# A mixer-and-MLP trunk in fp32 products of three matmuls: projections four k tiles ahead of the attention, the second half of q and k split earlier, and smaller edits to the first stage

## The chip, the cores and the metric

The kernel runs on one core of a Trainium2 chip. The metric is the device time of one execution in microseconds (us), lower is better, as the median of several runs. A profile of one execution, taken by the hardware profiler, goes with it. Differences of under 0.2% of the time, some 5 us, are not told apart here.

## What is computed

Two layers over a sequence of 1024 positions of width 1024, batch 1, all in float32. Layer 0 mixes tokens by forgetting attention (16 heads of 64), layer 1 by a chunked spatial gate; each is followed by a convolutional gated MLP of width 2816. The change lies in layer 0's first half:

```python
mod = silu(c) @ ada_w[0] + ada_b[0]            # shift, scale, gate, twice
h = rmsnorm(x, norm1_g[0]) * (1 + sc1) + sh1
q, k, v, o, fl = split(h @ w_in)               # q, k, v, o of width 1024, fl of 16
q, k = rmsnorm per head of 64, with gains
F = cumsum(log_sigmoid(fl + b_f))              # over positions
logits = q k^T / 8 + F[t] - F[s], causal
att = softmax(logits) @ v
x = x + gate * ((att * sigmoid(o)) @ w_out)
```

## The kernel before

TensorE multiplies float32 numbers that are split in two: `hi` is the number rounded to the format fp32r that TensorE reads, `lo` is the rest. `mm3` (L108) makes a product of three matmuls, hi by hi, hi by lo and lo by hi. `pair` and `split_lo` (L119 to L136) make the two parts: a copy on ACT, a subtraction on DVE. The cost of a split therefore falls on ACT and DVE, and TensorE waits for it where no other work lies ready.

**First stage.** `xn` holds the 8 row tiles of x. Each is squared on ACT with a sum (L319), groups of tiles then get their reciprocal root on DVE (`rstd`, `rsqrt`, L321 and L138, three Newton steps of small instructions), are scaled (L467) and transposed by TensorE (L469). `ada_first(q)` (L415), four times, multiplies a quarter of the first modulation matrix by `silu(c)` on DVE: eight row blocks of 512 columns, which arrive in two pieces of 1 MB or, for the tag `pt`, two halves of a piece. `raw_pieces` (L403) names the buffer for each of the 8 pieces. The buffers are those that the attention uses later (`qq`, `kh`, `kl`, `pt`) and the two of `w`; a piece that takes a buffer again has to wait until DVE has read the piece before. Then h is scaled, shifted and split (L494 to L496), and the o projections of three column blocks start (`acc`, L498).

**Attention.** Heads go in pairs, p = 0 to 7, two heads of 64 on the 128 partitions. For each pair `proj` (L566) makes q, k and v by 8 tiles of 128 positions in two halves, each tile a sum of 8 k tiles (three matmuls each, `pj`). After the fourth tile of a half, q and k are normalised: a square on ACT (L592), a sum on DVE (L594), the small Newton instructions, and a product on DVE (L600). `heads_qk(rw, half)` (L690) transposes q and k of a half into PSUM (`qk`), and splits them into `QQ`, `KH` and `KL`: per head a copy of q and one of k on ACT (L697), two subtractions on DVE (L699) and one more copy of k on ACT (L703). `scores(p, fb, qt)` (L731) multiplies one query tile with all keys so far, and makes the exponentials; query tiles 0 to 3 lie in the first half, 4 to 7 in the second. `values(p, g, hd, v)` (L781) transposes the probabilities (`ms`), splits them (L797 on ACT, L119 on DVE) and multiplies with v (`pv`).

What fills TensorE between these is a stream: the projections of the next pairs, then the output projection (`stream`, L664). `tick(w)` (L644) adds 0.85 w to `due` and takes one step, a k tile of three matmuls, for each whole unit. `until(p, half)` (L652) takes steps until that half of pair p is there. A pair's ticks come to 64.6 steps, its projection to 64, so the stream is neither much ahead nor behind. `KL` has halves of zeros, which are written once (L688): 16 pieces of 64 x 128.

The source order is not the order on the engines: a scheduler sets each engine's order when the program is built, from the source order and its own estimates. PSUM has 6 buffers for `pj`, `qk`, `s`, `pv` and `op` in rotation, and 2 for `ms`.

Of the kernel before, what the change touches and what calls it, by code (L numbers as in the profile page):

```python
# [8 lines left out]
F32 = mybir.dt.float32  # L9
# [3 lines left out]
AF = mybir.ActivationFunctionType  # L13
ALU = mybir.AluOpType
# [4 lines left out]
P = 128  # L19
# [48 lines left out]
class Trunk:  # L68
# [278 lines left out]
    def fox(self):  # L347
        nc, tc = self.nc, self.tc
# [7 lines left out]
        c = self.const  # L356

        with ExitStack() as es:
# [9 lines left out]
            def T(shape, dt, tag, bufs):  # L368
                return (mp if tag in ("qkv", "fraw") else fp).tile(shape, dt, tag=tag, name=self.name(tag), bufs=bufs)
# [31 lines left out]
            pieces = []  # L401

            def raw_pieces():  # L403

                pieces.append(0)
                if len(pieces) < 6:
                    nm = ("qq", "w", "kh", "kl", "w")[len(pieces) - 1]
                    return [self.wslot([P, 4, 2, 256], F32) if nm == "w" else T([P, 4, 2, 256], F32, nm, 1)]
                if len(pieces) % 4:
                    return [self.wslot([P, 4, 2, 256], F32)]  # L410
                return [T([P, 2, 2, 256], F32, "pt", 3) for _ in range(2)]

            a, sh = (T([P, KT], F32, nm, 1) for nm in ("a01", "sh01"))

# [37 lines left out]
            wo = []  # L452
            ht = {}
            rs = []
            for st0, n in ((0, 2), (2, 1), (3, 1), (4, 2), (6, 2)):
                ss = self.tile(self.small, [P, 4], F32, "n_ss")
                for i in range(n):
                    j = self.square(ss, i, xn[st0 + i], self.hslot(F32).rearrange("p a f -> p (a f)"))
                    if st0 + i == 0:
                        self.chain("act", j)  # L460
                r = self.rstd(ss, n)
                rs += [r[:, i : i + 1] for i in range(n)]
# [189 lines left out]
            def until(p, half):  # L652

                while len(rws[p]) <= half:
                    next(self.fill)
# [29 lines left out]
            own = [slice(hd * DH, (hd + 1) * DH) for hd in range(2)]  # L685
            for hd in range(2):
                for c in range(0, S, P):
                    nc.scalar.activation(KL[hd][own[1 - hd], c : c + P], self.ones[own[1 - hd]], AF.Copy, scale=0.0)  # L688

            def heads_qk(rw, half):  # L690
                hs = slice(half * 512, (half + 1) * 512)
# [28 lines left out]
            def f_rows(p):  # L720
                fb = []
                for hd in range(2):
                    t = T([P, S], F32, "fb", 2)
                    nc.sync.dma_start(t, nf[2 * p + hd].partition_broadcast(P))
                    fb.append(t)
                return fb
# [4 lines left out]
            def scores(p, fb, qt):  # L731

                nk = (qt + 1) * P
                sm = {}
                for hd in range(2):
                    d = u1()
                    col = qt * H + 2 * p + hd
                    nc.gpsimd.tensor_scalar(
                        d[:, :nk], fb[hd][:, :nk], -1.0, fq[:, col : col + 1], op0=ALU.mult, op1=ALU.add
                    )  # L740
                    last = d[:, nk - P : nk]
                    nc.gpsimd.affine_select(
                        out=last,
                        in_=last,
                        pattern=[[-1, P]],
                        compare_op=ALU.is_ge,
                        fill=NEG,
                        base=0,
                        channel_multiplier=1,
                    )  # L750
                    st_t[hd, qt] = d
                    sm[hd] = self.tile(self.small, [P, 2], F32, "smx")
                cuts = (0, nk) if nk <= 512 else (0, 512, nk)
                for j, (c0, c1) in enumerate(zip(cuts, cuts[1:])):
                    n = c1 - c0
                    pss = [ps1("s") for _ in range(2)]
                    for hd in range(2):
                        for i, k in enumerate((KH[hd], KL[hd])):
                            self.mm(pss[hd][:, :n], QQ[hd][:, qt * P : (qt + 1) * P], k[:, c0:c1], i == 0, i == 1)
                    for hd in range(2):  # L760
                        d = st_t[hd, qt][:, c0:c1]
                        nc.vector.tensor_tensor_reduce(
                            d, pss[hd][:, :n], d, -1.0, 3.4e38, ALU.add, ALU.min, sm[hd][:, j : j + 1]
                        )
                    tick(n / P)
                    flush()
                for hd in range(2):
                    d = st_t[hd, qt][:, :nk]
                    nm = sm[hd][:, 0:1]
                    if nk > 512:  # L770
                        nc.vector.tensor_tensor(nm, nm, sm[hd][:, 1:2], op=ALU.min)
                    l = self.tile(self.small, [P, 1], F32, "ll")
                    nc.scalar.activation(d, d, AF.Exp, bias=nm, scale=-1.0, accum_out=l)
                    r = self.tile(self.small, [P, 1], F32, "lr")
                    nc.vector.reciprocal(r, l)
                    if hd == 0:
                        nc.scalar.activation(d, d, AF.Copy, scale=r)
                    else:
                        nc.vector.tensor_scalar(d, d, r, None, op0=ALU.mult)
# [194 lines left out]

            self.fill = stream()
            next(self.fill)
            fb = f_rows(0)
            heads_qk(rws[0], 0)
            scores(0, fb, 0)
            v0 = None  # L980
            for p in range(8):
                if p:
                    values(p - 1, 3, 1, v0)
                v = self.wslot([P, NST, 256])
                heads_v(rws[p], v, 0)
                scores(p, fb, 1)
                until(p, 1)
                scores(p, fb, 2)
                values(p, 0, 0, v)
                scores(p, fb, 3)  # L990
                heads_qk(rws[p], 1)
                values(p, 0, 1, v)
                heads_v(rws[p], v, 1)
                scores(p, fb, 4)
                values(p, 1, 0, v)
                scores(p, fb, 5)
                values(p, 1, 1, v)
                scores(p, fb, 6)
                if p < 7:
                    until(p + 1, 0)  # L1000
                else:
                    flush()
                    while not done:
                        next(self.fill)
                    done.append(1)
                values(p, 2, 0, v)
                scores(p, fb, 7)
                values(p, 2, 1, v)
                if p < 7:
                    fb = f_rows(p + 1)  # L1010
                    heads_qk(rws[p + 1], 0)
                values(p, 3, 0, v)
                if p < 7:
                    scores(p + 1, fb, 0)
                v0 = v
# [977 lines left out]
```

## Time and profile before

| | |
|---|---|
| median of 3 runs (lowest to highest) | 2660.65 us (2659.45 to 2661.92) |
| the profiled execution: its time, its span | 2661.71 us, 2659.8 us |
| busy: TensorE (PE), weight loads (PEld), DVE, ACT, POOL | 96%, 82%, 78%, 55%, 6% |
| mean granted TensorE clock | 0.983 of full speed |
| HBM | 142 GB/s over the span |

The span runs from the first to the last instruction. Busy is the time in which an engine had an instruction under way; at its start each instruction may have waited, and the profile names what ended the wait. The clock column gives the share of full speed that TensorE was granted.

### The profile page before, as it was taken

Reading aid. Unit: us, or ns where it says so; the run is one execution under the profiler, and the core shown is the slowest. Engines: PE = TensorE matmul, PEld = TensorE weight load, DVE = VectorE, ACT = ScalarE, POOL = GpSimd, SP = SyncE. Lnnn points to the kernel's source line nnn. Section 1 sums busy time; section 2 is a strip of 40 time slices with the busy share of each in tenths; the row PEclk is TensorE's granted clock in tenths of the full one; section 3 lists DMA queues with packets and bytes.
Section 4 is the critical chain, followed back from the end, with each engine's and each line's share of the span. In section 5 each row is a group of like instructions: output and inputs, shape, how many; then the busy total and the mean of one; then the engine's idle time right before and its main releaser. Section 6 shows DMA issues by size and latency. Waiting matters only on the chain.

```text
span 2659.8 us, 35372 instructions
## 1 busy us (share of the span) xinstructions
PE 2565.9 (96%) x12578; PEld 2184.4 (82%) x12578; DVE 2072.6 (78%) x3597; ACT 1464.6 (55%) x2329; POOL 170.0 (6%) x289
## 2 busy tenths in 40 slices
PE   6999999998989999999999999999999999999997
PEld 5989988898778888888887888888887888888886
DVE  7677787888667998898678766666888988886875
ACT  7347666777555655455446644654466545455444
POOL 1122222222100000000000000000000000000000
PEclk8999999999999999999999999999999999999999
DMA  7751111112223354546645346557552344328462
GB/s 235 235 187 56 55 54 56 56 52 98 92 87 94 104 168 132 161 158 225 235 155 165 108 154 190 186 175 282 162 176 78 119 135 131 119 95 289 158 199 91
DMA packets 316520, 379.44 MB, mean 143 GB/s; under 512 B 18872, under 2 KB 196152, under 8 KB 316344
## 3 DMA queue, kind: packets, MB, share of 16 engines
q1 hardware_dynamic: 316120, 377.14, 43.7%
q8 instruction: 98, 1.61, 0.3%
q14 instruction: 78, 0.64, 0.1%
q10 hardware_dynamic: 224, 0.06, 0.0%
HBM read 287.41 MB, written 89.72 MB: 142 GB/s over the span
## 4 chain that ended last, share of the span: by engine, by line
PE 82%; DVE 8%; ACT 5%; DMA 3%; issue 2%; POOL 0%; SPq 0%; DVEq 0%; ACTq 0%; POOLq 0%
PE bankX L104 21%; PE banka L104 19%; PE bankY L104 17%; PE pj L104 7%; PE ms L104 5%; PE o L104 3%; PE ms L157 2%; PE s L104 2%; PE op L104 2%; PE pv L104 1%; PE ms L1815 1%; DVE ow L1146 1%; DVE pt L119 1%; DVE x L1146 1%; ACT pt L797 1%
## 5 line engine op out<-in xcount | busy, mean ns | idle before, releaser
L1133 ACT CAST ow<-rw 128x1024 fp32r<-128x1024 f32 (+1 forms) x438 | 397.9, 910 | 456.2 <-PE bankX L104 159.7
L1146 DVE TENSOR_TENSOR ow<-rw,ow 128x1024 fp32r<-128x1024 f32 (+1 forms) x438 | 456.5, 1045 | 146.3 <-ACT ow L1133 145.8
L104 PE MATMUL bankX<-hc,ow 128*128 128x512 f32 x1968 | 477.6, 391 | 1.0 <-DVE x L1146 0.7
L104 PEld LDWEIGHTS bankX<-hc,ow 128*128 128x128 f32 x1968 | 367.6, 188 | 78.6 <-DVE x L1146 1.7
L104 PE MATMUL banka<-hc,ow 128*128 128x512 f32 x1704 | 415.9, 393 | 1.3 <-DVE x L1146 1.3
L104 PEld LDWEIGHTS banka<-hc,ow 128*128 128x128 f32 x1704 | 319.6, 189 | 68.7 <-DVE x L1146 1.6
L104 PE MATMUL bankY<-hc,ow 128*128 128x512 f32 x1440 | 349.6, 391 | 0.0
L104 PEld LDWEIGHTS bankY<-hc,ow 128*128 128x128 f32 x1440 | 269.2, 188 | 55.8 <-issue 0.5
L104 PE MATMUL pj<-x,h 128*128 128x384 f32 (+1 forms) x1536 | 313.7, 345 | 0.2 <-DVE x L119 0.2
L104 PEld LDWEIGHTS pj<-x,h 128*128 128x128 f32 x1536 | 269.7, 191 | 5.0 <-DVE x L119 0.5
L1688 DVE SCALAR_TENSOR_TENSOR x<-x,prm,x 128x1022 f32<-128x1022 f32 (+1 forms) x160 | 203.9, 1279 | 2.5 <-ACT x L1686 2.0
L104 PE MATMUL bankY<-ow 128*128 128x512 f32 x720 | 203.5, 390 | 0.5 <-DVE x L1150 0.5
L104 PE MATMUL banka<-ow 128*128 128x512 f32 x672 | 187.4, 391 | 1.9 <-DVE x L1150 1.9
L104 PEld LDWEIGHTS bankY<-ow 128*128 128x128 f32 x720 | 134.6, 188 | 29.3 <-DVE x L1150 1.7
L104 PE MATMUL bankX<-ow 128*128 128x512 f32 x588 | 155.3, 390 | 0.0
L104 PEld LDWEIGHTS banka<-ow 128*128 128x128 f32 x672 | 125.7, 188 | 29.1 <-ACT x L1183 2.0
L104 PE MATMUL ms<-ow 128*128 128x512 f32 x546 | 140.0, 390 | 0.9 <-DVE pp L1146 0.9
L104 PE MATMUL pv<-pt,w 128*128 128x256 f32 (+1 forms) x640 | 119.9, 298 | 15.5 <-ACT pt L797 12.2
L119 DVE TENSOR_TENSOR pt<-ms,pt 128x512 fp32r<-128x512 f32 (+1 forms) x160 | 100.2, 632 | 40.6 <-ACT pt L797 38.8
L104 PEld LDWEIGHTS bankX<-ow 128*128 128x128 f32 x588 | 110.3, 188 | 23.4 <-issue 0.5
L797 ACT CAST pt<-ms 128x512 fp32r<-128x512 f32 (+1 forms) x160 | 85.3, 539 | 66.1 <-PE ms L157 55.2
L104 PEld LDWEIGHTS ms<-ow 128*128 128x128 f32 x546 | 102.0, 188 | 23.8 <-DVE pp L1146 2.9
(303 smaller groups left out, 3882.1 us busy)
## 6 DMA issues: line engine op xcount, KB each, us to landing
rw<-yd SPq DMA_DIRECT2D x210, 256.0 KB
rw<-in_ffn_w_up_dram SPq DMA_DIRECT2D x88, 512.0 KB
yd<-pp SPq DMA_DIRECT2D x60, 512.0 KB
rw<-in_ada_w_dram SPq DMA_DIRECT2D x48, 512.0 KB
rw<-in_ffn_w_down_dram SPq DMA_DIRECT2D x88, 256.0 KB
rw<-in_sgu_w_in_dram SPq DMA_DIRECT2D x32, 512.0 KB
yd<-x SPq DMA_DIRECT2D x30, 512.0 KB
fraw<-in_fox_w_in_dram SPq DMA_DIRECT2D x96, 128.0 KB
```

The source lines that it names most:

```text
L104: i = self.nc.tensor.matmul(out, lhsT, rhs, start=start, stop=stop, skip_group_check=self.strict)
L119: return (eng or self.nc.vector).tensor_tensor(lo, full, hi.bitcast(F32), op=ALU.subtract)
L157: i = self.nc.tensor.transpose(ps[: s.shape[1], j * P : (j + 1) * P], s, self.ident)
L797: nc.scalar.copy(pt[:, 0, :nb], ps[:, :nb])
L1133: return self.ao(self.nc.scalar.copy(t[:, 0], src))
L1146: return self.vo(self.nc.vector.tensor_tensor(out, a, b, op=op))
L1688: self.vo(stt(o[:, j:], a[:, : S - j], w[2 - j], o[:, j:], op0=ALU.mult, op1=ALU.add))
L1815: k = nc.tensor.matmul(px[:, b * P : (b + 1) * P], vn[:, b, c * P : (c + 1) * P], sg[:, 0], start=True, stop=True)
```

## The change

Five edits. (1) The pieces of the first modulation matrix take other buffers: pieces 6, 7 and 8 were `w`, `w` and `pt`, and are `pt`, `qq` and `w`. (2) The row tiles get their reciprocal roots in groups of 2, 2 and 4 where it was 2, 1, 1, 2 and 2. (3) The zeros of `KL` are written by GpSimd (POOL) where it was ACT. (4) Ahead of the first transposes of q and k, `due` is set to 4 and one `tick(0)` takes four steps of the stream, so all later steps come four k tiles earlier. (5) `heads_qk(rws[p], 1)` stands directly behind `until(p, 1)`, ahead of `scores(p, fb, 2)`; it stood behind `scores(p, fb, 3)`.

```diff
--- before.py
+++ after.py
@@ -402,13 +402,11 @@
 
             def raw_pieces():
 
-                pieces.append(0)
-                if len(pieces) < 6:
-                    nm = ("qq", "w", "kh", "kl", "w")[len(pieces) - 1]
-                    return [self.wslot([P, 4, 2, 256], F32) if nm == "w" else T([P, 4, 2, 256], F32, nm, 1)]
-                if len(pieces) % 4:
-                    return [self.wslot([P, 4, 2, 256], F32)]
-                return [T([P, 2, 2, 256], F32, "pt", 3) for _ in range(2)]
+                nm = ("qq", "w", "kh", "kl", "w", "pt", "qq", "w")[len(pieces)]
+                pieces.append(nm)
+                if nm == "pt":
+                    return [T([P, 2, 2, 256], F32, "pt", 3) for _ in range(2)]
+                return [self.wslot([P, 4, 2, 256], F32) if nm == "w" else T([P, 4, 2, 256], F32, nm, 1)]
 
             a, sh = (T([P, KT], F32, nm, 1) for nm in ("a01", "sh01"))
 
@@ -452,7 +450,7 @@
             wo = []
             ht = {}
             rs = []
-            for st0, n in ((0, 2), (2, 1), (3, 1), (4, 2), (6, 2)):
+            for st0, n in ((0, 2), (2, 2), (4, 4)):
                 ss = self.tile(self.small, [P, 4], F32, "n_ss")
                 for i in range(n):
                     j = self.square(ss, i, xn[st0 + i], self.hslot(F32).rearrange("p a f -> p (a f)"))
@@ -685,7 +683,9 @@
             own = [slice(hd * DH, (hd + 1) * DH) for hd in range(2)]
             for hd in range(2):
                 for c in range(0, S, P):
-                    nc.scalar.activation(KL[hd][own[1 - hd], c : c + P], self.ones[own[1 - hd]], AF.Copy, scale=0.0)
+                    nc.gpsimd.tensor_scalar(
+                        KL[hd][own[1 - hd], c : c + P], self.ones[own[1 - hd]], 0.0, None, op0=ALU.mult
+                    )
 
             def heads_qk(rw, half):
                 hs = slice(half * 512, (half + 1) * 512)
@@ -974,6 +974,9 @@
 
             self.fill = stream()
             next(self.fill)
+
+            self.due = 4.0
+            tick(0)
             fb = f_rows(0)
             heads_qk(rws[0], 0)
             scores(0, fb, 0)
@@ -985,10 +988,10 @@
                 heads_v(rws[p], v, 0)
                 scores(p, fb, 1)
                 until(p, 1)
+                heads_qk(rws[p], 1)
                 scores(p, fb, 2)
                 values(p, 0, 0, v)
                 scores(p, fb, 3)
-                heads_qk(rws[p], 1)
                 values(p, 0, 1, v)
                 heads_v(rws[p], v, 1)
                 scores(p, fb, 4)
```

Since the scheduler sets the order, these pieces show what became of it. In the names, `qk`, `s`, `pv`, `ms` and `pj` are as above, `qkv` is a half of q, k, v, and the numbers tell buffers apart.

TensorE before, head pair 1, from the transposes of the second half (`qk`) to the first scores that read it (`s_2815`, query tile 4):

```order
L157 MATMUL qk_2767<-ident,qkv_2165 128x128 x4
L157 MATMUL qk_2776<-ident,qkv_2165 128x128 x4
L104 MATMUL pv_2706<-pt_2711,w_2616 128x256
L104 MATMUL pv_2706<-pt_2711,w_2616 128x128 x2
L157 MATMUL ms_2869<-ident,cv_2667 128x128
L157 MATMUL ms_2869<-ident,cv_2720 128x128
L157 MATMUL ms_2869<-ident,cv_2667 128x128
L157 MATMUL ms_2869<-ident,cv_2720 128x128
L157 MATMUL ms_2883<-ident,cv_2667 128x128
L157 MATMUL ms_2883<-ident,cv_2720 128x128 x2
L104 MATMUL s_2815<-kh_745,qq_744 128x512
```

Between the transposes and those scores stood 3 `pv` and 7 transposes.

TensorE now, same pair, from the same transposes on:

```order
L157 MATMUL qk_2651<-ident,qkv_2097 128x128 x4
L157 MATMUL qk_2660<-ident,qkv_2097 128x128 x4
L104 MATMUL s_2683<-kh_717,qq_716 128x384
L104 MATMUL s_2683<-kl_718,qq_716 128x384
L104 MATMUL s_2684<-kh_717,qq_716 128x384
L104 MATMUL s_2684<-kl_718,qq_716 128x384
L104 MATMUL pj_2695<-x_2408,h_382 128x384 x3
L104 MATMUL pj_2695<-x_2411,h_402 128x384 x3
L104 MATMUL pj_2695<-x_2436,h_456 128x384 x3
L104 MATMUL pj_2695<-x_2439,h_494 128x384 x3
L104 MATMUL pj_2695<-x_2483,h_543 128x384 x2
L104 MATMUL s_2738<-kh_717,qq_716 128x512
```

Behind these stand 10 more `pj`, the second `s` pair of query tile 3, 4 `pv` and 2 transposes, and then the first scores of query tile 4 (`s_2801`): 24 `pj` and 8 matmuls of scores now lie between.

TensorE before, the same pair, the last rows ahead of the `qk` transposes; the projection of this half had ended 48 `pj`, 25 `pv` and 21 transposes earlier:

```order
L104 MATMUL pj_2744<-x_2548,h_571 128x384 x2
L104 MATMUL pv_2509<-pt_2573,w_1728 128x256
L104 MATMUL pj_2744<-x_2548,h_571 128x384
L104 MATMUL pj_2744<-x_2551,h_597 128x384 x2
L104 MATMUL pv_2509<-pt_2573,w_1728 128x256
L104 MATMUL pv_2509<-pt_2573,w_1728 128x128 x2
L157 MATMUL ms_2788<-ident,raw_2462 128x128
L157 MATMUL ms_2788<-ident,raw_2625 128x128 x2
L104 MATMUL pj_2744<-x_2551,h_597 128x384
L104 MATMUL pj_2744<-x_2579,h_623 128x384 x3
L104 MATMUL pj_2744<-x_2582,h_649 128x384 x2
L104 MATMUL pv_2706<-pt_2711,w_2616 128x256
```

Single `pj` and `pv` alternate up to the transposes.

TensorE now, the last rows ahead of the `qk` transposes; the projection of this half has ended 24 `pj`, 31 `pv`, 26 transposes and 6 matmuls of scores earlier (24 `pj` also in pairs 2 to 4, 48 in pairs 5 and 6):

```order
L157 MATMUL ms_2568<-ident,raw_2223 128x128
L104 MATMUL pv_2509<-pt_2515,w_1712 128x256 x3
L104 MATMUL pv_2509<-pt_2559,w_1712 128x256
L157 MATMUL ms_2583<-ident,raw_2105 128x128
L157 MATMUL ms_2583<-ident,raw_2223 128x128 x2
L104 MATMUL pv_2509<-pt_2559,w_1712 128x256 x3
L104 MATMUL pv_2509<-pt_2573,w_1712 128x256 x4
L157 MATMUL ms_2713<-ident,cv_2460 128x128
L157 MATMUL ms_2713<-ident,cv_2603 128x128 x2
L104 MATMUL pv_2509<-pt_2587,w_1712 128x256 x2
L104 MATMUL pv_2509<-pt_2587,w_1712 128x128 x2
L157 MATMUL ms_2772<-ident,raw_2466 128x128
```

The last 18 `pv` and 18 transposes ahead of `qk` now stand without a `pj` among them. On DVE, 32 rows stand from the sum of squares (L594) to the product that ends the normalisation (L600) of this half, before and now.

TensorE before, from the first transposes of q and k to the first scores:

```order
L281 MATMUL ms_1618<-ones,tm_1511 128x1 x4
L157 MATMUL qk_1678<-ident,qkv_807 128x128 x4
L281 MATMUL ms_1624<-ones,tm_1601 128x1 x4
L157 MATMUL qk_1687<-ident,qkv_807 128x128 x4
L104 MATMUL s_1710<-kh_745,qq_744 128x128
L104 MATMUL s_1710<-kl_746,qq_744 128x128
L104 MATMUL s_1711<-kh_745,qq_744 128x128
```

The scores followed the transposes directly.

TensorE now, the same place:

```order
L104 MATMUL pj_1645<-x_1622,h_456 128x384 x3
L104 MATMUL pj_1645<-x_1625,h_494 128x384 x3
L157 MATMUL qk_1662<-ident,qkv_779 128x128 x4
L157 MATMUL qk_1671<-ident,qkv_779 128x128 x4
L104 MATMUL pj_1645<-x_1632,h_543 128x384 x3
L104 MATMUL pj_1645<-x_1635,h_569 128x384 x3
L104 MATMUL pj_1645<-x_1638,h_595 128x384 x3
L104 MATMUL pj_1645<-x_1641,h_621 128x384 x3
L104 MATMUL s_1694<-kh_717,qq_716 128x128
```

12 `pj` stand between the transposes of q and k and the first scores.

## Rows read from the trace of the kernel before

**Rows 1.** The page, busy us of each engine, share of the span, instructions.

```profile
PE 2565.9 (96%) x12578; PEld 2184.4 (82%) x12578; DVE 2072.6 (78%) x3597; ACT 1464.6 (55%) x2329; POOL 170.0 (6%) x289
```

**Rows 2.** Busy us by stretch: PE, PEld, DVE, ACT, POOL, clock, DMA, GB/s.

```profile
0.00:66.00 66.00, 43.18 (x195) 33.58 (x196) 49.57 (x131) 46.47 (x90) 9.51 (x14) 0.90 0.75 236
...
190.00:680.00 490.00, 455.36 (x2839) 431.00 (x2838) 388.48 (x1111) 343.32 (x697) 127.48 (x218) 0.95 0.19 60
```

**Rows 3.** Waits of PE from 170 to 806 us: total, times, longest.

```profile
PE pv L104 <- ACT pt L797: 12.2, 10, 2.1
...
PE s L104 <- DVE qq L699: 5.5, 7, 2.2
```

**Rows 4.** PE in order of time, pair 1, at the second half's split.

```profile
261.81 1.04 PE L157 MATMUL qk<-ident,qkv 128*128 128x128 f32 x8
262.60 0.54 PE L104 MATMUL pv<-pt,w 128*128 128x256 f32 x3
262.97 0.95 PE L157 MATMUL ms<-ident,cv 128*128 128x128 f32 x7
264.09 0.50 PE L104 MATMUL s<-kh,qq 128*128 128x512 f32 x1 [0.17 <-DVE qq L699]
...
266.95 1.30 PE L157 MATMUL ms<-ident,raw 128*128 128x128 f32 x5 [2.13 <-DVE pt L119]
```

**Rows 5.** Seven such places, pairs 0 to 6 (196:199 to 608:615.2), summed.

```profile
sum 35.40, PE 17.59 PEld 10.22 DVE 33.60 ACT 34.27 POOL 17.20; mean PE 2.51 PEld 1.46 DVE 4.80 ACT 4.90 POOL 2.46
```

**Rows 6.** Ten stretches at half clock, 178 to 744.5 us: first; all summed.

```profile
178.00:184.60 6.60, 5.93 (x20) 5.74 (x21) 1.32 (x5) 3.38 (x6) 0.00 (x0) 0.50 0.00 0
...
sum 54.30, PE 47.89 PEld 41.40 DVE 39.06 ACT 32.68 POOL 17.60; mean PE 4.79 PEld 4.14 DVE 3.91 ACT 3.27 POOL 1.76
```

**Rows 7.** Groups by shape, 190 to 680 us: the split of q and k, ACT and DVE.

```profile
L697 ACT ACTIVATE qq<-qk,qg 64x512 fp32r<-64x512 f32 x28 | 19.1, 681 | 0.9 <-PE qk L157 0.3
...
L703 ACT CAST kh<-kh 64x512 fp32r<-64x512 f32 x28 | 17.3, 618 | 0.7
...
L699 DVE SCALAR_TENSOR_TENSOR qq<-qk,qg,qq 64x512 fp32r<-64x512 f32 x28 | 21.0, 750 | 6.2 <-ACT qq L697 5.4
```

**Rows 8.** The critical chain, a run of projection matmuls: start, us.

```profile
276.73 2.61 PE pj L104 x15
```

**Rows 9.** Last projection copy of a half to normalised q, k; pairs 1, 2.

```profile
245.52 0.47 ACT L586 COPY qkv<-pj 128x384 f32<-128x384 f32 x1
...
247.85 0.39 PE L104 MATMUL pv<-pt,w 128*128 128x256 f32 x1 [1.65 <-ACT pt L797]
...
256.98 1.25 DVE L600 TENSOR_TENSOR qkv<-qkv,rs_y 128x1024 f32<-128x1024 f32 x1
...
311.89 0.48 ACT L586 COPY qkv<-pj 128x384 f32<-128x384 f32 x1
...
325.73 1.21 DVE L600 TENSOR_TENSOR qkv<-qkv,rs_y 128x1024 f32<-128x1024 f32 x1
```

**Rows 10.** PE in order of time, the first scores of the attention.

```profile
177.94 0.47 PE L104 MATMUL s<-kh,qq 128*128 128x128 f32 x1 [2.12 <-ACT kh L703]
```

**Rows 11.** First stage in order of time; then groups, 0:60 and 0:680.

```profile
24.43 2.61 POOL L119 TENSOR_TENSOR x<-qkv,x 128x512 fp32r<-128x512 f32 x2 [22.89 <-ACT x L126]
...
25.76 1.83 DVE L433 SCALAR_TENSOR_TENSOR tm<-w,cact,tm 128x512 f32<-128x512 f32 x1
...
48.44 0.48 DVE L431 TENSOR_SCALAR tm<-w,cact 128x512 f32<-128x512 f32 x1 [1.40 <-DMA w<-in_ada_w_dram]
48.96 1.54 DVE L433 SCALAR_TENSOR_TENSOR tm<-w,cact,tm 128x512 f32<-128x512 f32 x2
...
L150 DVE SCALAR_TENSOR_TENSOR rs_y<-rs_t,rs_y 128x2 f32<-128x2 f32 x9 | 1.4, 155 | 0.1
...
L738 POOL TENSOR_SCALAR raw<-fb,fq 128x128 f32<-128x128 f32 x7 | 4.6, 660 | 64.6 <-DMA cv<-in_ada_w_dram 45.1 <-PE ms L157 12.8 <-DMA fb<-nf 6.7
...
L237 POOL MEMSET rows<- 128x128 f32 x5 | 0.9, 205 | 29.0 <-PE ms L157 29.0
```

## The prediction

> **What bounds the kernel.** The page comes first: TensorE is busy 96% of the span, the next engine, DVE, 78% [rows 1]. So time can only be won where TensorE waits, or where it runs at the lower of its two clock levels (1.2 GHz of 2.4, shown as 0.5). The table by stage says where: the first 66 us have 23 us without TensorE work, the stretch of the attention from 190 to 680 us has 490.0 - 455.4 = 34.6 us, and there the granted clock is 0.95 on average [rows 2]. The reader is to see that neither DVE (388 of 490 us) nor ACT (343) is full in the attention, so that TensorE's waits come from the order of the work and not from too much of it.
>
> Next come the waits by releaser. After 170 us TensorE waits for the probabilities' copies on ACT (12.2 us in 10 waits) and for the split of q on DVE (5.5 us) [rows 3]. In order of time, the second half's split is a cluster in every pair: `qk` at 261.81, then one short product and 7 transposes, then the scores wait for DVE's q, and the next transposes wait 2.13 us for DVE, which has the split's rows in front of the probabilities [rows 4]. The seven such places of pairs 0 to 6 hold 35.40 - 17.59 = 17.8 us without TensorE work [rows 5]. And the lower clock follows the waits: ten stretches between 178 and 744.5 us run at 0.5, 54.3 us in which TensorE was busy 47.9 us [rows 6]. At full clock that work takes half, so these stretches cost about 24 us. The one in the rows and six others open at the clusters or at the first scores; the last three open elsewhere.
>
> **The change, part by part.**
>
> *The earlier split (edit 5).* Per half it issues 6 instructions on ACT, 4 x 0.68 + 2 x 0.62 = 4.0 us, and 4 on DVE, 3.0 us [rows 7]. Before, about 1 us of TensorE work lay between the transposes and the scores that need them: 3 `pv` at (262.97 - 262.60) / 3 = 0.12 us and 7 transposes at (262.60 - 261.81) / 8 = 0.10 us [rows 4]. Now, by the order shown ahead, 24 `pj` lie there at 2.61 / 15 = 0.174 us [rows 8], 4.2 us, with scores, transposes and `pv` some 6.3 us. That is more than ACT's 4.0 us, so I take off the whole 17.8 us of [rows 5] for pairs 0 to 6. If the cover is gone, 2.5 us a pair come back. No DMA moves with it.
>
> *What is late next.* The same transposes now stand earlier against the normalisation that feeds them. Before, it took from the last copy of the half's projection (245.52) to the end of the product (256.98 + 1.25) 12.7 us in pair 1, and from 311.89 to 326.94, 15.1 us, in pair 2 [rows 9]; TensorE had 48 `pj` and more between and never waited. Now it has, in pairs 1 to 4, 24 x 0.174 + 31 x 0.12 + 26 x 0.10 us and 0.6 us for 6 small matmuls, about 11.1 us, and DVE has as many rows as before. So TensorE, and all that stands behind in its queue, waits 12.7 - 11.1 = 1.6 us at the least and 4.0 us at the most; I take 2.2, nearer the low end, since DVE's 32 rows there are as many as in pair 1's case. Pairs 5 and 6 have 48 `pj` there and pair 7 the output projection, so they don't wait. That is 4 x 2.2 = 8.8 us new. In exchange a wait goes: the `pv` that stood behind the square on ACT (1.65 us at 247.85) [rows 9] is of the kind that waited 12.2 / 10 = 1.2 us on average [rows 3], one in each of these pairs, 4.9 us, and it now lies inside the stretch that DVE bounds. Net +3.9 us.
>
> *Four k tiles ahead (edit 4).* It moves work and adds none: 12 `pj`, 12 x 0.174 = 2.1 us, fill the 2.12 us that TensorE waited at the first scores [rows 10]. I take off 2.1 us. It also gives the earlier split its only cover: without it the pairs' transposes would come 12 `pj` sooner behind the projection.
>
> *The clock.* Seven of the ten half-clock stretches belong to waits that go; the new waits in four pairs will bring about four back. So 3 of 10 of 24 us, 7 us, come off; the ends are 0 and 17.
>
> *New waits that I can't place.* The split's 4.0 us on ACT and 3.0 us on DVE now stand ahead of exponentials and copies that earlier ones fed. I put a quarter of the 17.8 us back, 4.5 us, as a judgement; the ends are 0 and the rival below.
>
> *First stage (edits 1 to 3).* Groups of 2, 2 and 4 need 39 small DVE instructions where it was 59; 20 x 0.155 = 3.1 us off DVE [rows 11], which is busy 49.6 of the first 66 us [rows 2]. Tiles 4 to 7 must all be there first, which gives part of it back. The buffers end the wait of DVE for a late piece, 1.40 us [rows 11]. The zeros leave ACT, which was not the bound. On GpSimd no row shows them; the nearest are a memset of 128 x 128, 0.205 us, and a multiply and add of that size, 0.66 us with neighbours [rows 11], so 16 take 3.3 to 10.6 us. While GpSimd subtracted for 2.6 us from 24.43, a DVE accumulation took 1.83 us [rows 11], against 1.54 us for two of them at 48.96 with GpSimd idle. So zeros on GpSimd can hold DVE. I take 3.5 us for that, the low end, since the zeros are half as high and DVE's other rows run between; the sum is 3.5 - 3.1 - 1.4 = -1.0 us, with ends at +6 (10.6) and -5.
>
> The Trainium skill has a rule that speaks against this edit (SBUF — State Buffer, Who interferes with whom): a DVE instruction with two SBUF inputs contends with a GpSimd instruction that reads SBUF, and the one that comes second waits for the whole of the other. The zeros read `ones`, so they are of that kind, where a memset would not be; the 1.83 us row agrees. By the rule the term is nearer +6 than -1, and the sum below -12.5 in place of -19.5.
>
> *Sum.* -17.8 + 3.9 - 2.1 - 7 + 4.5 - 1.0 = -19.5 us. The profiled execution took 2661.7 us, 1.0 us over the median of the runs, so 2642 us there and **2641 us** as a median. The matmuls and the stages after 806 us are the same.
>
> **The rivals.**
>
> *The wait only moves.* If the normalisation takes pair 2's 15.1 us in all of pairs 1 to 4, the new waits are 16 us, 11 us net, and no stretch of low clock goes: -17.8 + 11.1 - 2.1 + 4.5 - 1.0 = -5.3 us, 2655 us. For it speaks that the last 18 `pv` and 18 transposes ahead of the split now stand without `pj`; against it, that pair 2 is the longer of the two cases shown.
>
> *GpSimd holds DVE in the first stage.* At the high end the first stage gains +6 instead of -1: 2648 us. Against it: from 52 us on TensorE has work ahead, so that only part of DVE's lateness reaches the end.
>
> *Slower: the split stands in front of the values.* Its place is `values(p, 0, 0)`: if ACT has no gap between the six copies and the first copy of the probabilities, each of pairs 1 to 7 waits the full 4.0 us, 7 x 4.0 = 28 us in place of the 4.5, and the clock gives nothing back: -17.8 + 3.9 - 2.1 + 28 - 1.0 = +11 us, 2672 us. It decides from a wait of about 2.5 us a pair on. Against it: ACT is idle 147 of 490 us, some 20 us a pair [rows 2], and 14 `pj` stand directly behind the next scores.
>
> *The change does nothing here.* The scheduler could have ordered both the same. The order shown ahead says otherwise; what is left is that the chip's waits sit where the order did not change, 2660 us.
>
> **How the numbers follow.** Forecast 0.57, the wait only moves 0.20, GpSimd holds DVE 0.10, slower 0.09, nothing 0.04. A measurement here can tell 0.2%, 5.3 us, from no change: faster means under 2655.3. The forecast, the GpSimd case and about half of the moved wait, less a little for what I can't place, give 0.75 faster; the other half of the moved wait and the case of nothing give 0.15 same; 0.10 slower. The low end of the range is the sum with the clock at its end (-17), the new waits at 1.6 us a pair and no unplaced ones, and the first stage at -3: -17.8 + 1.5 - 2.1 - 17 - 3 = -38, 2622 us. The high end, 2658 us, takes in the moved wait and leaves out the slower case.
>
> **What would show it.** Right: no wait of `s` for DVE's q at the second half, `pj` in those places; new waits of the `qk` transposes for DVE's L600 product of 1.5 to 4 us in pairs 1 to 4 and none in 5 to 7; fewer half-clock stretches between 178 and 745 us; the first scores about 2 us sooner after their transposes. Wrong: `pv` waits for ACT that grow past 12 us by more than 10, `qk` waits in all pairs, or DVE rows in the first stage that stretch beside GpSimd's zeros.

## The result, and the profile after

The changed kernel takes **2637.99 us** (median of 4 runs, 2635.54 to 2639.01), the kernel before beside it 2660.31 us (4 runs, 2659.45 to 2661.92). The ratio is 0.9914, 95% interval 0.9902 to 0.9926: 22 us faster. The forecast was 2641 us, its range 2622 to 2658. The sum behind it does not hold term by term: the attention gained more than forecast, and the first stage lost where a small gain was forecast.

The page after, same columns as [rows 1]:

```profile
PE 2552.9 (97%) x12578; PEld 2176.1 (83%) x12578; DVE 2074.0 (79%) x3577; ACT 1461.9 (55%) x2313; POOL 183.7 (7%) x305
```

TensorE has 13.0 us less busy time for the same 12578 matmuls, at a mean clock of 0.988 instead of 0.983. To place the rest, I cut each span at the first transposes of q and k and behind the last `pv`. The table by stretch, columns as in [rows 2], of the kernel before:

```profile
0.00:173.90 173.90, 151.08 (x740) 129.59 (x741) 124.17 (x284) 79.47 (x154) 26.30 (x46) 0.96 0.76 245
173.90:795.80 621.90, 576.92 (x3503) 534.75 (x3502) 470.32 (x1309) 419.89 (x844) 143.73 (x244) 0.95 0.21 66
795.80:2659.80 1864.00, 1837.93 (x8338) 1520.03 (x8337) 1478.05 (x2004) 965.20 (x1334) 0.00 (x0) 0.99 0.49 159
```

and of the changed kernel:

```profile
0.00:184.80 184.80, 155.80 (x760) 135.01 (x761) 128.14 (x267) 76.66 (x138) 38.28 (x63) 0.94 0.72 235
184.80:773.70 588.90, 560.53 (x3483) 522.22 (x3481) 467.22 (x1306) 419.71 (x843) 145.37 (x242) 0.98 0.22 68
773.70:2635.80 1862.10, 1836.59 (x8337) 1518.88 (x8337) 1478.60 (x2004) 965.57 (x1333) 0.00 (x0) 1.00 0.49 159
```

The parts change by +10.9, -33.0 and -1.9 us, together the -24.0 of the two spans. Twenty matmuls now stand ahead of the cut (760 where there were 740): 12 `pj` of edit 4, 2.1 us, and 8 small sums (`ms<-ones,tm`, L281), some 0.8 us. Without them the first stage is 8.0 us later and the attention 30.1 us shorter. In the attention TensorE's idle time falls from 45.0 to 28.4 us and its busy time by 16.4 us, 2.9 of them moved work, most of the rest the clock.

TensorE's waits after, from 170 to 806 us, as in [rows 3]:

```profile
PE pv L104 <- ACT pt L797: 8.6, 12, 2.1
PE s L104 <- ACT kh L703: 4.7, 2, 3.5
PE qk L157 <- DVE qkv L598: 3.5, 4, 1.7
PE ms L157 <- DVE pt L119: 3.4, 8, 0.7
```

In the kernel before, the last of these rows was:

```profile
PE ms L157 <- DVE pt L119: 11.4, 13, 2.2
```

The wait of `s` for DVE's q (5.5 us) is gone, the next transposes wait 8.0 us less for DVE's probabilities, and the forecast new wait of `qk` is there, four times. (The first-stage edits shift the lines: L598 is the L600 of before, L431 was L433, L686 was L688, L465 was L467.) TensorE in order of time at pair 1, as in [rows 4]:

```profile
263.01 1.97 PE L157 MATMUL qk<-ident,qkv 128*128 128x128 f32 x8 [1.70 <-DVE qkv L598]
264.63 0.67 PE L104 MATMUL s<-kh,qq 128*128 128x384 f32 x1
...
266.06 2.67 PE L104 MATMUL pj<-x,h 128*128 128x384 f32 x14
268.57 0.39 PE L104 MATMUL s<-kh,qq 128*128 128x512 f32 x1
```

The other three waits are 0.66, 0.53 and 0.66 us, in pairs 2 to 4; pairs 5 to 7 have none. Half-clock stretches between 170 and 810 us, the first and the sum of six, as in [rows 6]:

```profile
191.10:197.90 6.80, 6.23 (x24) 6.14 (x25) 4.27 (x18) 5.63 (x14) 0.98 (x2) 0.50 0.00 0
...
sum 23.80, PE 22.36 PEld 20.87 DVE 19.01 ACT 16.31 POOL 3.56; mean PE 3.73 PEld 3.48 DVE 3.17 ACT 2.72 POOL 0.59
```

Before there were twelve in this range (the ten of [rows 6] and two of 3.4 us behind them), 61.1 us.

The first stage, GpSimd, then DVE, then TensorE in order of time (compare [rows 11]):

```profile
35.40 11.25 POOL L686 TENSOR_SCALAR kl<-ones 64x128 fp32r<-64x128 f32 x16 [7.95 <-DVE tm L431]
46.63 5.43 POOL L119 TENSOR_TENSOR x<-qkv,x 128x512 fp32r<-128x512 f32 x4
...
40.50 0.78 DVE L431 SCALAR_TENSOR_TENSOR tm<-pt,cact,tm 128x512 f32<-128x512 f32 x1
...
44.71 1.24 DVE L441 SCALAR_TENSOR_TENSOR a<-a,prm 128x2 f32<-128x2 f32 x1
45.88 5.07 DVE L431 SCALAR_TENSOR_TENSOR tm<-qq,cact,tm 128x512 f32<-128x512 f32 x1
50.98 1.63 DVE L431 SCALAR_TENSOR_TENSOR tm<-qq,cact,tm 128x512 f32<-128x512 f32 x1
52.65 0.75 DVE L431 SCALAR_TENSOR_TENSOR tm<-qq,cact,tm 128x512 f32<-128x512 f32 x1
...
29.99 1.84 PE L104 MATMUL ms<-ones,tm 128*128 128x1 f32 x8 [7.78 <-DVE tm L431]
...
55.64 12.05 PE L104 MATMUL o<-h,x 128*128 128x512 f32 x40 [4.69 <-DVE h L119]
```

The zeros take 11.25 us. Most of them barely touch DVE (0.78 us for an accumulation at 40.50, against half of 1.54 [rows 11]); beside the last ones a small step of 128 x 2 takes 1.24 us, where the same step at 54.11 takes 0.15. GpSimd's four subtractions stand behind the zeros and start at 46.63 instead of 42.25. The accumulation that DVE begins at 45.88, beside the last zeros, ends only behind the third subtraction, after 5.07 us; the next one takes 1.63 us. In the four other runs below that multiply on GpSimd (first_only, newton_old, buffers_old, no_split) one accumulation takes 4.6 to 4.9 us there; in the kernel before the longest beside these subtractions takes 1.86. TensorE waits for the split of h until 55.64, where it went on at 52.74 before.

### The profile page after: what moved, and what is told of

Same layout as the page of the kernel before. It is cut to its first block, busy times and chain, and to the rows that moved or that the text cites. A ratio compares the mean times of both kernels' runs of the same rounds, so it can differ in the third digit from the quotient of the medians.

```text
span 2635.8 us, 35388 instructions
## 1 busy us (share of the span) xinstructions
PE 2552.9 (97%) x12578; PEld 2176.1 (83%) x12578; DVE 2074.0 (79%) x3577; ACT 1461.9 (55%) x2313; POOL 183.7 (7%) x305
## 4 chain that ended last, share of the span: by engine, by line
PE 86%; DVE 6%; ACT 3%; DMA 2%; issue 2%; SPq 0%; DVEq 0%; ACTq 0%
PE bankX L104 21%; PE banka L104 19%; PE bankY L104 18%; PE pj L104 9%; PE ms L104 5%; PE o L104 3%; PE ms L157 3%; PE s L104 2%; PE op L104 2%; PE pv L104 2%; PE ms L1818 1%; DVE ow L1149 1%; PE ms L281 1%; PE qk L157 1%; DVE x L1149 1%
## 5 line engine op out<-in xcount | busy, mean ns | idle before, releaser
L104 PEld LDWEIGHTS pv<-pt,w 128*128 128x128 f32 x640 | 96.5, 191 | 20.2 <-ACT pt L797 12.9
## 6 DMA issues: line engine op xcount, KB each, us to landing
rw<-yd SPq DMA_DIRECT2D x210, 256.0 KB
rw<-in_ffn_w_down_dram SPq DMA_DIRECT2D x88, 256.0 KB
```

What stands on the lines that cost most here:

```text
L104: i = self.nc.tensor.matmul(out, lhsT, rhs, start=start, stop=stop, skip_group_check=self.strict)
```

## The experiments

Each kernel was timed in five rounds beside the kernel before (its medians 2658.3 to 2660.4 us), so ratios are compared. **The first four** take the change apart. Theory A came from the two traces: the attention edits gain about 30 us, the first stage loses about 7.

**attention_only**, edits 4 and 5 in the kernel before:

```diff
+            self.due = 4.0
+            tick(0)
             fb = f_rows(0)
...
                 until(p, 1)
+                heads_qk(rws[p], 1)
                 scores(p, fb, 2)
                 values(p, 0, 0, v)
                 scores(p, fb, 3)
-                heads_qk(rws[p], 1)
```

> Edits 4 and 5 alone; the first stage is that of before. Theory A (the attention gained about 30 us, the first stage lost about 7): 2660 - 30 = 2630 us, with PE busy 43 of the first 66 us as before and the half-clock stretches between 178 and 745 us as few as in the change. Rival B (the first stage costs nothing, its later end is made up behind it): 2638 us, as the whole change. Rival C (the forecast's own terms, attention -18.5, first stage -4): 2642 us.

2643.32 us, ratio 0.9936 (0.9923 to 0.9949): 16 us faster, not 30. By its time only rival C fits, but that rival had the first stage gain.

**first_only**, edits 1 to 3 in the kernel before:

```diff
-            for st0, n in ((0, 2), (2, 1), (3, 1), (4, 2), (6, 2)):
+            for st0, n in ((0, 2), (2, 2), (4, 4)):
...
-                    nc.scalar.activation(KL[hd][own[1 - hd], c : c + P], self.ones[own[1 - hd]], AF.Copy, scale=0.0)
+                    nc.gpsimd.tensor_scalar(
+                        KL[hd][own[1 - hd], c : c + P], self.ones[own[1 - hd]], 0.0, None, op0=ALU.mult
+                    )
```

(and the buffers of edit 1).

> Edits 1 to 3 alone; the attention's source is that of before. Theory A: 2660 + 7 = 2667 us. Rival B: 2660 us. Rival C: 2656 us or less. In all three the clusters of the second half's split, with waits of s for DVE's q of some 5 us, are there as before.

2667.74 us, 1.0032 (1.0022 to 1.0042): 8.7 us slower, as theory A had it. Rivals B and C fall. But 0.9936 x 1.0032 is 0.9968, and the whole change measures 0.9914. The parts do not add up: about 14 us (9 to 20 by the intervals) are won only where both are in. Nor is all of the 8.7 us lost ahead of the attention: in first_only's profile the first transposes come 4.3 us late, and the attention, whose order on TensorE is that of before but for a few rows, is 4.0 us longer, with some 7 us more at half clock between 170 and 810 us.

**split_only**, edit 5 alone (attention_only without the two lines on `due`):

> Edit 5 without edit 4. If the four k tiles ahead are the cover of the transposes (the forecast's step), 12 pj at 0.174 us are missing ahead of them: 2.1 us more wait for L600 in each of pairs 1 to 4, where the change waited 0.5 to 1.7 us, so 8 us over edits 4 and 5 together, some 2638 us. Rival: DVE is early enough anyway and the stream's place is of no account, within 2 us of edits 4 and 5 together, some 2630 us.

2645.56 us, 0.9943 (0.9929 to 0.9956), against 0.9936 with both. The interval allows the rival's difference and not the 8 us. Its trace does show the cover missing in pair 1, where `qk` waited 4.46 us, but the sum of such waits is 8.8 us in six places, against 9.8 us in attention_only.

**ahead_only**, edit 4 alone (attention_only without the moved `heads_qk`):

> Edit 4 without edit 5. The clusters of the second half's split stay. By the forecast's term it takes 2.1 us off: 2658 us. Rival, from the trace of the change (the first scores' wait was 3.5 us with 12 pj ahead of them): nothing, 2660 us.

2650.89 us, 0.9963 (0.9950 to 0.9975): 8 us, more than either expected. The clusters stay, and there `s` waits 2.4 us for DVE's q instead of 5.5. At the first scores the second head still waits 3.5 us. In its profile the attention is 600.4 us where it was 621.9, but the part behind it is 8.7 us longer: there the first matmul of the MLP (`bankX`) waits 4.1 us for DVE, where before it waited 0.3.

**The next four** undo one first-stage edit at a time in the changed kernel.

**zeros_act**:

```diff
-                    nc.gpsimd.tensor_scalar(
-                        KL[hd][own[1 - hd], c : c + P], self.ones[own[1 - hd]], 0.0, None, op0=ALU.mult
-                    )
+                    nc.scalar.activation(KL[hd][own[1 - hd], c : c + P], self.ones[own[1 - hd]], AF.Copy, scale=0.0)
```

> The whole change without edit 3: the zeros of KL are written by ACT again. Theory A (the 11.25 us of zeros on GpSimd hold its four subtractions of the next o weights until DVE's accumulations, which then take 2.5 us each instead of 0.75): the first stage loses nothing from it, 2638 - 6 = 2632 us, and GpSimd's four subtractions end near 48 us instead of 52. Rival N (the group of four roots, whose four scalings stand in front of the first quarter's accumulations, is the loss): 2638 us, no change.

2635.47 us, 0.9910 (0.9897 to 0.9923). This is not told apart from the change, and the 6 us of theory A are not there. GpSimd's subtractions ended at 50.4 us, and the first transposes came at 180.3 us where the change had 184.8, so the profile shows a sooner first stage and the time does not. (The 2.5 us each that theory A gives is the mean of the three accumulations of 5.07, 1.63 and 0.75 us.)

**newton_old**:

```diff
-            for st0, n in ((0, 2), (2, 2), (4, 4)):
+            for st0, n in ((0, 2), (2, 1), (3, 1), (4, 2), (6, 2)):
```

> The whole change without edit 2: groups of 2, 1, 1, 2, 2 again. Theory A: the first quarter's transposes come 2.2 us sooner, the zeros still hold the rest: within 2 us of the whole change, 2636 to 2638 us. Rival N (the group of four is the loss): 2638 - 6 = 2632 us.

2639.72 us, 0.9922 (0.9908 to 0.9935). Rival N falls: the group of four alone is not the loss.

**buffers_old**, the function `raw_pieces` of before in the changed kernel:

```diff
-                nm = ("qq", "w", "kh", "kl", "w", "pt", "qq", "w")[len(pieces)]
...
+                if len(pieces) % 4:
+                    return [self.wslot([P, 4, 2, 256], F32)]
+                return [T([P, 2, 2, 256], F32, "pt", 3) for _ in range(2)]
```

> The whole change without edit 1: the last three pieces of the modulation matrix take the buffers of before. By the forecast DVE waits 1.4 us for a late piece again: 2639 us. Rival (the pieces in qq and pt are late or are held in the change): 2634 us or less.

2639.86 us, 0.9926 (0.9913 to 0.9940): by the ratios 3 us above the change and not told apart from it. That fits the forecast's term and does not show it, since 1.4 us are less than these runs resolve. Its rival falls.

**zeros_memset**:

```diff
-                    nc.gpsimd.tensor_scalar(
-                        KL[hd][own[1 - hd], c : c + P], self.ones[own[1 - hd]], 0.0, None, op0=ALU.mult
-                    )
+                    nc.gpsimd.memset(KL[hd][own[1 - hd], c : c + P].bitcast(F32), 0.0)
```

> The whole change with the zeros on GpSimd as memsets of the same 16 pieces, which read nothing. If a piece goes by the memset row of before (0.2 us for 128 x 128), the zeros take 3.3 us instead of 11.25 and the four subtractions start 8 us sooner: 2632 us, as with the zeros on ACT. Rival: a memset of 64 rows costs as much as the multiplication, 0.7 us: 2638 us.

2633.95 us, 0.9905 (0.9889 to 0.9921): the lowest median of all, but its interval overlaps the change's. GpSimd and DVE in order of time:

```profile
35.30 2.78 POOL L686 MEMSET kl<- 64x128 f32 x16 [7.90 <-DVE tm L431]
42.28 6.19 POOL L119 TENSOR_TENSOR x<-qkv,x 128x512 fp32r<-128x512 f32 x4 [4.21 <-issue]
...
47.18 3.41 DVE L431 SCALAR_TENSOR_TENSOR tm<-qq,cact,tm 128x512 f32<-128x512 f32 x3
```

The expected 2632 us and the rival's 2638 both lie within the interval; the trace decides for the first. The zeros take a quarter of the time, the subtractions start at 42.28 as before the change, and the three accumulations take 3.41 us together instead of 7.52. The first transposes come at 177.1 us, 7.7 us sooner than in the change; the time shows 2 us of that, less than these runs resolve.

**The last four** look for the 14 us. In a program with the source of edits 4 and 5, the scheduler wrote two different orders of the attention: attention_only and the whole change differ there in some 610 rows of TensorE, counted in both lists, some 310 in each. The scheduler works with estimates of time; theory O is that the first-stage edits shift them.

**newton_attention**, attention_only with one line of the first stage:

```diff
-            for st0, n in ((0, 2), (2, 1), (3, 1), (4, 2), (6, 2)):
+            for st0, n in ((0, 2), (2, 2), (4, 4)):
```

> Edits 2, 4 and 5: attention_only with the Newton groups of the change. On TensorE its order is that of the whole change but for 16 rows of the first stage, while attention_only (edits 4 and 5) differs from the change in 610 rows of the attention, though the source there is the same. Theory O (the first stage's edits shift the scheduler's own clock, so it writes another order of the attention, and that order is worth the 10 us or so that are missing in attention_only): 2632 us, with about 3.5 us of waits of qk for L600 and some 24 us at half clock between 170 and 810 us, where attention_only had 9.8 and 54. Rival (the buffers and the zeros bring it): 2643 us, as attention_only.

2635.59 us, 0.9906 (0.9890 to 0.9923), where attention_only had 0.9936 (0.9923 to 0.9949): 8 us between them. In the attention its order on TensorE is that of the whole change. Theory O holds. The middle part of the table by stretch, attention_only:

```profile
176.10:783.10 607.00, 571.07 (x3482) 529.85 (x3480) 472.07 (x1306) 420.48 (x843) 145.42 (x242) 0.96 0.20 66
```

and newton_attention:

```profile
179.10:770.90 591.80, 563.00 (x3482) 522.91 (x3480) 467.24 (x1306) 420.00 (x842) 145.22 (x242) 0.98 0.21 68
```

These are 15.2 us for the same work, though the line was put in the first stage: 7.1 us of TensorE's idle time and 8.1 us of busy time. The times show less, for two reasons: attention_only's profile is of its slowest run (2649.03 us, its median 2643.32), and newton_attention's first part is 3.0 us longer. Four profiles with the change's order (the change, newton_attention, zeros_act, buffers_old) have 588.6 to 595.8 us here. Pair 2 shows where the two orders part. ACT, DVE, GpSimd and TensorE, attention_only:

```profile
309.63 0.48 ACT L586 COPY qkv<-pj 128x384 f32<-128x384 f32 x1
...
321.70 0.75 DVE L148 TENSOR_TENSOR rs_t<-rs_y 128x16 f32<-128x16 f32 x1
...
322.74 0.64 DVE L150 SCALAR_TENSOR_TENSOR rs_y<-rs_t,rs_y 128x16 f32<-128x16 f32 x1
...
324.64 0.65 DVE L149 TENSOR_TENSOR rs_t<-rs_t,rs_vh 128x16 f32<-128x16 f32 x1
...
326.40 1.22 DVE L600 TENSOR_TENSOR qkv<-qkv,rs_y 128x1024 f32<-128x1024 f32 x1
...
321.63 0.80 POOL L738 TENSOR_SCALAR raw<-fb,fq 128x640 f32<-128x640 f32 x1
...
322.67 1.46 POOL L738 TENSOR_SCALAR cv<-fb,fq 128x512 f32<-128x512 f32 x2
...
324.37 0.90 POOL L738 TENSOR_SCALAR raw<-fb,fq 128x768 f32<-128x768 f32 x1
...
327.68 1.97 PE L157 MATMUL qk<-ident,qkv 128*128 128x128 f32 x8 [5.23 <-DVE qkv L600]
```

and newton_attention:

```profile
308.99 0.49 ACT L586 COPY qkv<-pj 128x384 f32<-128x384 f32 x1
...
320.17 0.17 DVE L149 TENSOR_TENSOR rs_t<-rs_t,rs_vh 128x16 f32<-128x16 f32 x1
...
322.36 1.23 DVE L600 TENSOR_TENSOR qkv<-qkv,rs_y 128x1024 f32<-128x1024 f32 x1
...
323.64 1.09 PE L157 MATMUL qk<-ident,qkv 128*128 128x128 f32 x8 [0.66 <-DVE qkv L600]
```

From the last copy of the projection to the end of the product, attention_only takes 18.0 us and newton_attention 14.6. In the first, Newton steps that take 0.16 us alone come behind the start of GpSimd's multiply-and-adds (L738) and end with them, after 0.64 to 0.75 us. The three shown make about 1.6 of the 3.4 us; what makes the rest, with other rows in between, is not shown. In the second the last steps fall between those instructions and keep 0.16 to 0.21 us, and it is GpSimd that is held: its L738 of 128 x 640 beside the product takes 1.88 us, 0.80 in the rows above. The waits of `qk` come to 9.8 us in the one and 3.5 in the other. At some of these waits the clock falls. In attention_only it falls in pair 1, where `ms` waits 2.94 us for DVE (L779) and `qk` 0.86 (half clock from 253.7 us), and at the `qk` waits of 5.23 and 3.04 us in pairs 2 and 3 (from 325.4 and 397.1), but not at pair 4's of 0.65 us. In newton_attention it falls at pair 1's alone, 1.71 us (from 255.5). Yet zeros_memset has pair 1's wait too, 1.70 us at 256.0, and the granted clock there is 1.00 from 189.1 to 571.4 us. In sum 54.4 us are at half clock in attention_only against 30.6, 17.0 against 3.4 of them at these places.

**no_split**, the change without edit 5:

```diff
                 until(p, 1)
-                heads_qk(rws[p], 1)
                 scores(p, fb, 2)
                 values(p, 0, 0, v)
                 scores(p, fb, 3)
+                heads_qk(rws[p], 1)
```

> The whole change without edit 5. By the forecast's terms for that edit (-17.8 + 3.9 + 4.5 - 7 = -16.4): 2638 + 16 = 2654 us, with s waiting for DVE's q some 5 us again. Rival (edit 4 alone already brought 8 us and edit 5 on top of it 8): 2646 us.

2659.07 us, 0.9995 (0.9985 to 1.0005): no gain at all. Edit 5 is worth 21 us in the whole change, more than both expected, and not all of it in the attention: by the profiles the change is 14.8 us shorter there (588.9 for 603.7) and 11.2 us shorter behind it, where no_split's `bankX` waits 4.1 us for DVE (0.3 in the change), while the change's first transposes come 3.7 us later. And what edit 4 gives alone (0.9963) the first stage takes (0.9963 x 1.0032 = 0.9995). So these two do add up. `s` waits 2.4 us for DVE's q, not 5 as expected; edit 4 had halved that wait in ahead_only too.

**ahead_8** and **ahead_12**, zeros_memset with another number in one line:

```diff
-            self.due = 4.0
+            self.due = 8.0
```

> zeros_memset (all five edits, the zeros as memsets) with the stream eight k tiles ahead instead of four. The transposes of the second half then have 48 pj in pairs 1 to 6 between them and the end of the projection (30 in pair 0, 38 in pair 4) where they had 24. If the cover is what counts: no waits of qk for L600 (3.5 us before) and fewer half-clock stretches, 2634 - 4 to 8 = 2626 to 2630 us. Rival (what is taken ahead is missing later, and DVE becomes the wait of pv and ms): 2634 us or more.

2642.87 us, 0.9936 (0.9919 to 0.9952).

> The same with twelve k tiles ahead: 48 pj or more in every pair. If the cover is what counts, as with eight: 2626 to 2630 us. Rival: the last pair, which has no projection of its own left, runs out of fillers earlier and the waits of pv for ACT grow: 2636 us or more.

2637.92 us, 0.9919 (0.9905 to 0.9934). In both no wait of `qk` for L598 is left, as the cover theory said, and neither is faster than zeros_memset, as the rivals said. In ahead_8 the waits move to `s` for ACT's k (8.1 us where zeros_memset had 5.2) and `pv` for DVE (6.9 where it had 3.0), and 44.3 us are at half clock where it had 27.2. In ahead_12 the attention is 586.5 us instead of 591.5, but it has lost 48 matmuls, 24 `pj` (4.2 us) to the part ahead of it and 24 matmuls to the part behind it, which is 8.3 us longer. The rival's mechanism for ahead_12, `pv` waiting for ACT, is wrong: 4.8 us where zeros_memset had 10.5.

## Why the prediction was right, step by step

The time was right by luck, because two errors offset each other: the attention became 30.1 us shorter where 18.5 were forecast, and the first stage 8.0 us longer where a gain of 1.0 was.

- **Earlier split, -17.8.** Right in mechanism and place: no `s` waits for DVE's q at the second half, and `pj` stand there. The waits that it names fell by 13.5 us, `s` for DVE's q from 5.5 to none and `ms` for DVE's probabilities from 11.4 to 3.4. It is the edit that carries the change (no_split), in part behind the attention, where the forecast had nothing.
- **New waits of `qk`, +8.8.** Right in place (pairs 1 to 4, none in 5 to 7), too large: 3.5 us. Both ends of that difference were off. In the changed kernel's pair 2 the normalisation runs from 316.16 to 330.75, 14.6 us and not 12.7, and TensorE's own work and small waits there filled 13.9 us and not 11.1. My least of 1.6 us a pair was no bound: three of the four stayed under it. In attention_only the same source waits 9.8 us, so this term depends on the order that the scheduler wrote.
- **Waits that go, -4.9, and unplaced ones, +4.5.** `pv` waits for ACT fell from 12.2 to 8.6 us; nothing of the unplaced waits is seen in the table of waits. Taken together, the idle terms (-17.8 + 3.9 - 2.1 + 4.5 = -11.5) became -16.6.
- **Four k tiles ahead, -2.1.** Failed at the place it names; the edit alone brought 8 us (ahead_only), and there the waits at the clusters were shorter. The first scores of the first head come 3.0 us behind the first transposes instead of 4.0 and no longer wait, but the second head's do, at 191.67. TensorE, then ACT, of the changed kernel:

```profile
191.67 0.48 PE L104 MATMUL s<-kh,qq 128*128 128x128 f32 x1 [3.54 <-ACT kh L703]
...
189.19 1.28 ACT L773 ACT_TABLE_LOAD   x1
...
191.00 0.62 ACT L703 CAST kh<-kh 64x512 fp32r<-64x512 f32 x1
```

  ACT loads a table and makes the first head's exponential ahead of the last copy of k; before, the copy at 178.62 stood ahead of the table load at 179.26. I counted the matmuls that fill the wait and not what stands in front of the copy on ACT. That the 12 `pj` are the split's only cover was not shown either: split_only and attention_only are not told apart.
- **The clock, -7.** Too small. TensorE worked 47.9 us in the ten stretches of before and 22.4 us in the six of after: half of the difference, 12.8 us, came back. The forecast put about four stretches at the new waits; only the one at 262.7 came, and the others were 0.5 to 0.7 us. That a new wait brings a stretch with it was not certain either: zeros_memset waits 1.70 us at the same place at full clock.
- **First stage, -1.0.** Failed: 8.7 us (5.9 to 11.2) as a time in first_only, 8.0 us to the first transposes in the profile of the change, where the ends were +6 and -5. The step that failed is the price of the zeros: I asked how far they hold DVE (3.5 us) and took the low end of 3.3 to 10.6 us. They took 11.25 us, held DVE beside the last ones, and delayed what is queued behind them on GpSimd, which held DVE for longer. So one of the signs of being wrong, DVE rows that stretch beside GpSimd's zeros, came in part. What this path costs in time is not shown: with the zeros on ACT again (zeros_act) the time is not told apart. The group of four was booked as a gain of 3.1 us of DVE; its four scalings stand together, and the first quarter's sums (`ms<-ones,tm`) start at 29.99 instead of 27.74. How the 8.7 us divide stays open: no single undoing differs from the change beyond its interval, and three profiles with this first stage (first_only, no_split, the change) have their first transposes 4.3, 4.3 and 8.0 us late, counted without the 20 matmuls in the two that have them.

By rows the rival on GpSimd had the right place and about the right price, in part by another path. The moved wait and the slower case did not come: the `pv` waits did not grow. The forecast missed altogether that the edits act on each other: the first stage changes the order of the attention. That order is worth 8 us (2 to 14) by the times of newton_attention and attention_only, of some 14 that the parts leave open.

## What to carry to other kernels

Where a scheduler orders the program, take a change apart and put it together again: here the parts gave 0.9968, the whole 0.9914, and at least part of the 14 us between them lay in an order that one line far ahead had shifted. When work moves to an idle engine, price what is queued behind it there: the trace shows that here, though the times do not resolve it. And a short wait can cost more than itself where the clock falls with it: at the waits of pairs 1 to 3 attention_only had 17.0 us at half clock, newton_attention 3.4. Not every such wait brings that: zeros_memset's of 1.70 us did not.

## What the runs showed of the hardware

- Sixteen multiplications of 64 x 128 on GpSimd took 11.25 us (0.70 each on average), sixteen memsets of the same pieces 2.78 us (0.17 each).
- What GpSimd does decides how far DVE is held. Beside most of the multiplications a DVE accumulation took 0.78 us, but beside the last ones a step of 0.15 us took 1.24, and in first_only an accumulation that ran beside zeros alone (at 45.33) took 1.65. Beside GpSimd's subtractions, one behind the other, an accumulation took 5.07 us in the change and 4.6 to 4.9 in four other runs, so it was held while several GpSimd instructions went by; why the next GpSimd instruction came first is not shown. Beside GpSimd's multiply-and-adds in the attention a Newton step of 0.16 us took 0.64 to 0.75 us, and beside DVE's product one of these took 1.88 us instead of 0.80. The Trainium skill (SBUF — State Buffer, Who interferes with whom) says that a DVE instruction with two SBUF inputs contends with a GpSimd instruction that reads SBUF. The Newton steps, the accumulations beside the subtractions and the 1.24 and 1.65 us beside the last zeros agree; the 0.78 us beside the earlier zeros, which read `ones` too, shows almost nothing of it.
- The same first stage showed 23.9, 17.1 and 13.6 us at half clock in its first 100 us in three profiles (the change, first_only, no_split), so one profile's term there is good to some microseconds only.
